# Readout gate, merge gates and both branch products with tokens on the output partitions

## The chip, the cores and the metric

The kernel runs on one core of a Trainium2 chip. The time is what one execution takes on the device in microseconds (us). TensorE (PE) multiplies: it loads a stationary operand of 128x128 (PEld) and streams a moving operand of up to 512 columns through it, into a PSUM bank. There are eight banks of 128 x 512 in fp32. DVE is VectorE, ACT is ScalarE, POOL is GpSimd and SP is the queue that issues most of the loads.

## The reference

One layer of a diffusion backbone on 256 latent tokens with 256 context tokens, width 2048, all in fp32. What matters here, with `h` the normed and modulated latent tokens and `p_g`, `p_gc`, `p_gh` columns of the one input projection `h @ w_in`:

```
o = rms_norm(o, hgrn_norm_g)                      # per head of 128
y_h = (o * silu(p_g)) @ hgrn_out_w                # 1024 -> 2048, "who"
y_c = silu(layer_norm(conv(u))) @ conv_pw_w       # 1024 -> 2048, "wpw"
z = sigmoid(p_gc) * y_c + sigmoid(p_gh) * y_h
y = z @ w_out                                     # 2048 -> 2048, "wo"
x = x + ga_m * rms_norm(y, norm_post_mix)         # then the squared-ReLU MLP, 2048 -> 8192 -> 2048
```

## The kernel before

Each fp32 operand is split into a high part (rounded to `fp32r`) and a low part, and a product takes three terms: high x high, high x low and low x high. Weights come from HBM as tiles of 128 x 1024 (512 KB). For each tile ACT writes the high part (`whi`, L84) and DVE the low part (`wlo`, L85). `Stream.next` (L87 on) prepares them four tiles ahead (`AHEAD`), with four buffers each for `whi` and `wlo` and five for the raw tile. Between the weights the stream carries tiles of the modulation weights (`add_gemv`, the side stream), each of which is consumed by one DVE instruction (L779 or L790).

There are two ways of multiplying. In `blocks`, a block of 128 output features is the stationary operand and the 256 tokens move. `mm2` multiplies the high weight with high and low tokens side by side (512 columns, L197) and then the low weight with the high tokens (256 columns, L198), so the bank holds two halves of 256 that `total` adds up: an ACT copy (L176) and a DVE add (L177). In `tokens`, 128 tokens are the stationary operand and 512 weight columns move. `mm3r` issues three matmuls of 512 columns (L203 to L205) for two halves of the tokens and two halves of the tile, in four banks. A group is one pass over all the input features for 1024 output features. Its last three tiles (`LAST`; six at the end of a chain, `END`) are run bank by bank, so that the first banks are complete while the last ones are still being filled. The second MLP product and `wo` were already done this way.

The stages around the change run in this order: the conv gate and the conv value, the readout gate `g` (8 blocks of 128 features), the merge gates for conv and hgrn (16 blocks each), `who` (16 blocks with 8 input blocks), `wpw` (the same), and `wo`. In the first three of the changed stages the moving or stationary operand is `hlat`, the latent tokens; `who` reads the readout's result `self.rp`, `wpw` the conv branch's result `self.cv`. Both lie in the first halves of the pages that hold the latent tokens.

Background work is written as generators and lets itself be advanced by `pump(us)`: a pump adds a credit, and each step that a generator yields costs some of it. At most three generators (`LIVE`) are advanced. In this stretch they are the conv branch (steps of four DVE instructions, L990, at 1.6 a step, then a layer norm with two means on TensorE, L1013), two readouts of four heads each (with transposes on TensorE, L973), and gain rows that follow a completed side product (L828). `finish` advances one to its end. A planner puts each engine's instructions in order from these priorities and its own estimate of durations. An engine runs its queue in that order. `page` gives one of 30 buffers of 128 x 1024; the loads of x for the residual (L633, on the POOL queue) wait for four of them to be free.

Of the kernel before, what the change touches and what calls it, by code (L numbers as in the profile page):

```python
# [8 lines left out]
F32 = mybir.dt.float32  # L9
# [6 lines left out]
P = 128  # L16
# [79 lines left out]
class Kernel:  # L96
# [141 lines left out]
    def tokens(self, x, evac, us, end=False):  # L238


        for g in range(2):
            n = KT - (END if end and g else LAST)
            accs = [self.bank() for _ in range(4)]

            def part(w, k, tb, j):
                xh, xl = x(k)[:2]
                t, c = slice(tb * P, (tb + 1) * P), slice(j * 512, (j + 1) * 512)
                self.mm3r(accs[2 * tb + j], (xh[:, t], xl[:, t]), (w[0][:, c], w[1][:, c]), k == 0, k == KT - 1)
            for k in range(n):
                w = self.stream.next(AHEAD)  # L250
                for tb in range(2):
                    for j in range(2):
                        part(w, k, tb, j)
                self.pump(us)
            ws = [self.stream.next(min(AHEAD, KT - k) if end and g else AHEAD) for k in range(n, KT)]
            for tb in range(2):
                for j in range(2):
                    for k, w in enumerate(ws):
                        part(w, n + k, tb, j)
            for tb in range(2):  # L260
                for j in range(2):
                    evac(tb, 2 * g + j, accs[2 * tb + j])
            self.pump(us)
# [22 lines left out]
    def run(self):  # L286
# [91 lines left out]
        for b in [*range(40, 48), *range(32, 40), *range(24, 32), *range(48, 80)]:  # L378
            w_in(b)
            if b % 7 < 3:  # L380
                gemv(1)
# [201 lines left out]
        def ev_g(b, accs):  # L583
            acc = self.totals(accs, self.small(512, "sum"))
            sg = self.small(512, "sg")
            nc.scalar.activation(out=sg, in_=acc, func=AF.Sigmoid)
            for j in range(2):
                s = slice(j * T, (j + 1) * T)
                nc.vector.scalar_tensor_tensor(self.at(self.sg, b + j), acc[:, s], v["hng"][:, b + j:b + j + 1], sg[:, s], op0=ALU.mult, op1=ALU.mult)

        self.blocks(8, hlat, KT, ev_g, 1.1)
# [4 lines left out]
        gp = [[], []]  # L596

        def ev_gate(i):
            def ev(b, accs):
                if b % PB == 0:  # L600
                    gp[i].append(self.page(F32, "gate"))
                acc = self.totals(accs, self.at(gp[i], b, 2))
                nc.scalar.activation(out=acc, in_=acc, func=AF.Sigmoid)
            return ev

        self.blocks(16, hlat, KT, ev_gate(0), 1.1)
        self.blocks(16, hlat, KT, ev_gate(1), 1.1)
# [4 lines left out]
        def ev_ho(b, accs):  # L612
            acc = self.totals(accs, self.small(512, "sum"))
            y = self.at(gp[1], b, 2)
            nc.vector.tensor_tensor(y, acc, y, op=ALU.mult)

        self.blocks(16, self.operand(self.rp), 8, ev_ho, 1.2)
# [3 lines left out]
        def ev_pw(b, accs):  # L621
            acc = self.totals(accs, self.small(512, "sum"))
            z, y = self.at(gp[0], b, 2), self.at(gp[1], b, 2)
            nc.vector.tensor_tensor(z, acc, z, op=ALU.mult)
            nc.vector.tensor_tensor(z, z, y, op=ALU.add)
            self.split(z, self.at(zh, b, 2), self.at(zl, b, 2))

        self.blocks(16, self.operand(self.cv), 8, ev_pw, 1.2)


# [38 lines left out]
        self.tokens(zx, ev_wo, 1.4, end=True)  # L669
# [287 lines left out]
    def readout(self, j):  # L957

        nc = self.nc
        while self.ended < 4 * (j + 1):  # L960
            yield None
        r = self.osq[:, 8 * j:8 * j + 8]
        self.rstd(r, r, 1.0 / P)
        for h in range(4 * j, 4 * j + 4):
            o = self.at(self.on, h)
            for tb in range(2):
                s = o[:, tb * P:(tb + 1) * P]
                nc.vector.tensor_scalar(out=s, in0=s, scalar1=self.osq[:, 2 * h + tb:2 * h + tb + 1], scalar2=None, op0=ALU.mult)
            yield 0.4
            yield None  # L970
            ps = self.bank()
            for tb in range(2):
                nc.tensor.transpose(out=ps[:, tb * P:(tb + 1) * P], in_=o[:, tb * P:(tb + 1) * P], identity=self.v["ident"])  # L973
            nc.vector.tensor_tensor(o, ps[:, :T], self.at(self.sg, h), op=ALU.mult)
            self.split_parts(o, self.rp, h, 1)
            yield 0.8

    def conv(self, uhv, uvv):
# [74 lines left out]
       ("wm0", (64, P, TW), F32), ("crow", (2, TW), F32), ("wmt", (64, P, TW), F32), ("wm1", (64, P, TW), F32), ("wi0", (16, P, TW), F32), ("wi1", (160, P, TW), F32),  # L1053
       ("wpw", (16, P, TW), F32), ("who", (16, P, TW), F32), ("wo", (32, P, TW), F32), ("w1", (128, P, TW), F32), ("w2", (128, P, TW), F32)]
# [76 lines left out]
```

## Time and profile before

| | us |
|---|---|
| median of 3 runs | 1710.58 (1710.08 to 1710.60) |
| profiled execution | 1710.51 |
| its span, first to last instruction | 1708.7 |
| PE busy | 1669.4 |
| PEld busy | 1418.5 |
| DVE busy | 1205.3 |
| ACT busy | 869.9 |
| DMA | 374.61 MB, mean 219 GB/s |

The page's share of busy time is an average over stages with different limits. A matmul's row shows its duration with what overlaps the next one, so a pace is read from the distance of two starts in the timeline. "Idle before" is the time that an engine stood still ahead of an instruction, and the name behind the arrow is what ended it.

### The profile page before, as it was taken

The page shows a single profiled execution, that of the slowest core. Times are in us where ns is not written, and L with a number is a line of the kernel's source. Part 1 is how long each engine was busy: PE and PEld are TensorE (multiplying, and loading weights), DVE is VectorE, ACT ScalarE, POOL GpSimd, SP SyncE. Part 2 cuts the span into 40 slices and gives each one's busy share as a digit, 9 for nine tenths or more (in the row PEclk, how much of TensorE's full clock was granted, in tenths as well). Part 3 has the DMA queues.
Part 4 walks back from the last instruction along what each step waited for, and adds up shares of the span by engine and source line. Part 5 has one row for each costly group of instructions (what it writes and reads, how often), then busy time and mean ns, then how long its engine had stood idle before and what let it go on. Part 6 is the DMA issues. An engine that isn't in the chain of part 4 may idle for free.

```text
span 1708.7 us, 24005 instructions
## 1 busy us (share of the span) xinstructions
PE 1669.4 (98%) x9082; PEld 1418.5 (83%) x9082; DVE 1205.3 (71%) x1688; ACT 869.9 (51%) x1260; POOL 8.1 (0%) x18
## 2 busy tenths in 40 slices
PE   4999999999999999999999999999999999999997
PEld 2777887888888888888888898888888888888886
DVE  6887767777676999997797566555665665556555
ACT  8785333344454444574455466445553455345542
POOL 0000000000000000000000000000000000000000
PEclk9999999999999999999999999999999999999999
DMA  8887985433356677668887466767666666766553
GB/s 326 309 298 283 335 270 166 148 124 111 99 166 205 208 236 237 221 215 277 294 268 260 150 209 221 213 227 229 219 216 218 233 221 211 228 219 196 193 190 120
DMA packets 103348, 374.61 MB, mean 219 GB/s; under 512 B 11584, under 2 KB 11584, under 8 KB 103232
## 3 DMA queue, kind: packets, MB, share of 16 engines
q1 hardware_dynamic: 101952, 368.86, 65.2%
q0 software_dynamic: 1280, 4.21, 0.7%
q8 instruction: 71, 1.16, 0.3%
q14 instruction: 45, 0.37, 0.1%
HBM read 370.93 MB, written 2.10 MB: 218 GB/s over the span
## 4 chain that ended last, share of the span: by engine, by line
PE 86%; DMA 5%; DVE 4%; ACT 3%; issue 2%; SPq 0%; DVEq 0%; ACTq 0%
PE bank L197 27%; PE bank L198 14%; PE bank L204 8%; PE bank L205 8%; PE bank L203 8%; PE bank L192 4%; PE bank L190 4%; PE bank L191 4%; DMA raw<-wm 4%; PE bank L905 2%; DVE wlo L85 2%; PE bank L849 1%; PE bank L848 1%; PE bank L847 1%; ACT whi L84 1%
## 5 line engine op out<-in xcount | busy, mean ns | idle before, releaser
L85 DVE TENSOR_TENSOR wlo<-raw,whi 128x1024 fp32r<-128x1024 f32 x547 | 665.3, 1222 | 315.3 <-ACT whi L84 309.2
L84 ACT ACTIVATE whi<-raw 128x1024 fp32r<-128x1024 f32 x547 | 575.6, 1059 | 599.5 <-PE bank L197 227.6
L197 PE MATMUL bank<-h,whi 128*128 128x512 f32 x2176 | 766.6, 397 | 0.0
L198 PE MATMUL bank<-h,wlo 128*128 128x256 f32 x2176 | 610.9, 281 | 3.3 <-DVE wlo L85 3.2
L197 PEld LDWEIGHTS bank<-h,whi 128*128 128x128 f32 x2176 | 408.3, 188 | 95.5
L198 PEld LDWEIGHTS bank<-h,wlo 128*128 128x128 f32 x2176 | 411.5, 189 | 4.9 <-DVE wlo L85 4.7
L204 PE MATMUL bank<-wlo,hidh 128*128 128x512 f32 x500 | 194.6, 389 | 0.0
L203 PE MATMUL bank<-whi,hidh 128*128 128x512 f32 x500 | 194.6, 389 | 0.0
L205 PE MATMUL bank<-whi,hidl 128*128 128x512 f32 x500 | 194.6, 389 | 0.0
L190 PE MATMUL bank<-h,whi 128*128 128x512 f32 (+1 forms) x384 | 140.7, 367 | 1.8 <-ACT whi L84 1.0
L191 PE MATMUL bank<-h,whi 128*128 128x512 f32 (+1 forms) x384 | 136.1, 355 | 0.0
L192 PE MATMUL bank<-h,wlo 128*128 128x512 f32 (+1 forms) x384 | 135.8, 355 | 0.0
L205 PEld LDWEIGHTS bank<-whi,hidl 128*128 128x128 f32 x500 | 93.9, 188 | 19.6
L203 PEld LDWEIGHTS bank<-whi,hidh 128*128 128x128 f32 x500 | 93.9, 188 | 19.5
L204 PEld LDWEIGHTS bank<-wlo,hidh 128*128 128x128 f32 x500 | 93.9, 188 | 19.3
L779 DVE SCALAR_TENSOR_TENSOR gacc<-raw,silu_c,gacc 128x1024 f32<-128x1024 f32 x60 | 76.9, 1282 | 46.3 <-DMA raw<-wm 46.0
L790 DVE SCALAR_TENSOR_TENSOR raw<-raw,silu_row 128x1024 f32<-128x1024 f32 x64 | 77.3, 1221 | 25.8 <-DMA raw<-wmt 25.8
L485 PE MATMUL bank<-whi,s 128*4 128x256 f32 x256 | 66.9, 294 | 16.8 <-ACT whi L84 16.8
L190 PEld LDWEIGHTS bank<-h,whi 128*128 128x128 f32 x384 | 72.8, 190 | 10.7 <-ACT whi L84 1.2
L192 PEld LDWEIGHTS bank<-h,wlo 128*128 128x128 f32 x384 | 72.3, 189 | 10.5 <-DVE wlo L85 0.2
L191 PEld LDWEIGHTS bank<-h,whi 128*128 128x128 f32 x384 | 72.8, 190 | 8.6 <-DVE h L185 0.3
L486 PE MATMUL bank<-wlo,s 128*4 128x256 f32 x256 | 66.0, 291 | 6.9 <-DVE wlo L85 6.3
(203 smaller groups left out, 1538.5 us busy)
## 6 DMA issues: line engine op xcount, KB each, us to landing
raw<-w SPq DMA_DIRECT2D x256, 512.0 KB, 4.2
raw<-wi SPq DMA_DIRECT2D x176, 512.0 KB, 4.3
raw<-wm SPq DMA_DIRECT2D x128, 512.0 KB, 4.6
raw<-wmt SPq DMA_DIRECT2D x64, 512.0 KB, 4.4
raw<-wo SPq DMA_DIRECT2D x32, 512.0 KB, 4.5
raw<-who SPq DMA_DIRECT2D x16, 512.0 KB, 4.7
raw<-wpw SPq DMA_DIRECT2D x16, 512.0 KB, 4.5
x<-x SPq DMA_DIRECT2D x4, 512.0 KB, 7.3
```

The lines of the kernel that those rows point to most:

```text
L84: nc.scalar.activation(out=hi, in_=raw, func=AF.Copy)
L85: kn.los.append(nc.vector.tensor_tensor(lo, raw, hi.bitcast(F32), op=ALU.subtract))
L190: nc.tensor.matmul(out, w[0], x[0], start=first, stop=False)
L191: nc.tensor.matmul(out, w[0], x[1], start=False, stop=False)
L192: nc.tensor.matmul(out, w[1], x[0], start=False, stop=last)
L197: nc.tensor.matmul(bank, w[0], x[2], start=first, stop=False)
L198: nc.tensor.matmul(bank[:, T:], w[1], x[0], start=False, stop=last)
L203: nc.tensor.matmul(out, x[0], w[0], start=first, stop=False)
L204: nc.tensor.matmul(out, x[0], w[1], start=False, stop=False)
L205: nc.tensor.matmul(out, x[1], w[0], start=False, stop=last)
L779: nc.vector.scalar_tensor_tensor(acc, raw, s, acc, op0=ALU.mult, op1=ALU.add)
L790: nc.vector.scalar_tensor_tensor(raw, raw, 1.0, self.srow, op0=ALU.mult, op1=ALU.mult, accum_out=self.dot[:, 32 * j + b:32 * j + b + 1])
```

## The change

The readout gate, the merge gates and the products `who` and `wpw` go from `blocks` to `tokens`. Their weights are laid out in rows (new input `wi2`, and `who` and `wpw` by `rows`). `tokens` gets the number of input blocks (`nk`), the number of groups, another order of the four banks (`pairs`) and a hook before a tile (`pre`). The gates are now evacuated from the bank by one sigmoid. The norm gain moves from the gate's evacuation to the readout, and the gate is multiplied before the readout's transpose instead of after it. The merged result z has tokens on partitions, so `turn_z` transposes it in eight steps of four 128x128 transposes, four steps during the second group of `wpw` and four during the first group of `wo`, and splits each step's bank into high and low part. The pumps of these stages have 1.3 in place of 1.1 and 1.2, one per tile outside the last three, and one per group. The order of `w_in` columns in the stream and the places of the side stream's tiles are rewritten to fit. The cut hunk declares the shapes of the inputs.

```diff
--- before.py
+++ after.py
@@ -235,31 +235,33 @@
             evac(2 * j, accs[j])
         self.pump(us)
-    def tokens(self, x, evac, us, end=False):
-        for g in range(2):
-            n = KT - (END if end and g else LAST)
+    def tokens(self, x, evac, us, end=False, nk=KT, groups=2, pairs=False, pre=None):
+        order = [(tb, j) for j in range(2) for tb in range(2)] if pairs else [(tb, j) for tb in range(2) for j in range(2)]
+        for g in range(groups):
+            last = end and g == groups - 1
+            n = nk - (END if last else LAST)
             accs = [self.bank() for _ in range(4)]
             def part(w, k, tb, j):
                 xh, xl = x(k)[:2]
                 t, c = slice(tb * P, (tb + 1) * P), slice(j * 512, (j + 1) * 512)
-                self.mm3r(accs[2 * tb + j], (xh[:, t], xl[:, t]), (w[0][:, c], w[1][:, c]), k == 0, k == KT - 1)
+                self.mm3r(accs[2 * tb + j], (xh[:, t], xl[:, t]), (w[0][:, c], w[1][:, c]), k == 0, k == nk - 1)
             for k in range(n):
+                if pre is not None:
+                    pre(g, k)
                 w = self.stream.next(AHEAD)
-                for tb in range(2):
-                    for j in range(2):
-                        part(w, k, tb, j)
+                for tb, j in order:
+                    part(w, k, tb, j)
                 self.pump(us)
-            ws = [self.stream.next(min(AHEAD, KT - k) if end and g else AHEAD) for k in range(n, KT)]
-            for tb in range(2):
-                for j in range(2):
-                    for k, w in enumerate(ws):
-                        part(w, n + k, tb, j)
-            for tb in range(2):
-                for j in range(2):
-                    evac(tb, 2 * g + j, accs[2 * tb + j])
+            ws = [self.stream.next(min(AHEAD, nk - k) if last else AHEAD) for k in range(n, nk)]
+            for tb, j in order:
+                for k, w in enumerate(ws):
+                    part(w, n + k, tb, j)
+            for tb, j in order:
+                evac(tb, 2 * g + j, accs[2 * tb + j])
             self.pump(us)
     def cut(self, pages, tb, c):
@@ -375,9 +377,13 @@
             gemv(1 + (h + 1) % 2)
             w_in(8 + h)
             gemv(1 + (h + 1) % 2)
-        for b in [*range(40, 48), *range(32, 40), *range(24, 32), *range(48, 80)]:
+        for b in [*range(32, 40), *range(24, 32)]:
             w_in(b)
             if b % 7 < 3:
+                gemv(1)
+        for b in range(80):
+            st.add(a["wi2"][b])
+            if b % 14 < 6 and b % 2 == 0:
                 gemv(1)
         for nm in ("who", "wpw"):
             for b in range(16):
@@ -580,52 +586,65 @@
         self.sg = self.pages(2, F32, "silu_g")
-        def ev_g(b, accs):
-            acc = self.totals(accs, self.small(512, "sum"))
-            sg = self.small(512, "sg")
-            nc.scalar.activation(out=sg, in_=acc, func=AF.Sigmoid)
-            for j in range(2):
-                s = slice(j * T, (j + 1) * T)
-                nc.vector.scalar_tensor_tensor(self.at(self.sg, b + j), acc[:, s], v["hng"][:, b + j:b + j + 1], sg[:, s], op0=ALU.mult, op1=ALU.mult)
-        self.blocks(8, hlat, KT, ev_g, 1.1)
+        def ev_g(tb, c, acc):
+            s = self.sg[tb][:, c * 512:(c + 1) * 512]
+            nc.scalar.activation(out=s, in_=acc, func=AF.Sigmoid)
+            nc.vector.tensor_tensor(s, acc, s, op=ALU.mult)
+        self.tokens(hlat, ev_g, 1.3, groups=1)
         for j in range(2):
             heads.append(self.push(self.readout(j)))
-        gp = [[], []]
+        gp = [[None] * 4, [None] * 4]
         def ev_gate(i):
-            def ev(b, accs):
-                if b % PB == 0:
-                    gp[i].append(self.page(F32, "gate"))
-                acc = self.totals(accs, self.at(gp[i], b, 2))
-                nc.scalar.activation(out=acc, in_=acc, func=AF.Sigmoid)
+            def ev(tb, c, acc):
+                if c % 2 == 0:
+                    gp[i][2 * tb + c // 2] = self.page(F32, "gate")
+                nc.scalar.activation(out=self.cut(gp[i], tb, c), in_=acc, func=AF.Sigmoid)
             return ev
-        self.blocks(16, hlat, KT, ev_gate(0), 1.1)
-        self.blocks(16, hlat, KT, ev_gate(1), 1.1)
+        self.tokens(hlat, ev_gate(0), 1.3)
+        self.tokens(hlat, ev_gate(1), 1.3)
         for g in heads:
             self.finish(g)
-        def ev_ho(b, accs):
-            acc = self.totals(accs, self.small(512, "sum"))
-            y = self.at(gp[1], b, 2)
+        def ev_ho(tb, c, acc):
+            y = self.cut(gp[1], tb, c)
             nc.vector.tensor_tensor(y, acc, y, op=ALU.mult)
-        self.blocks(16, self.operand(self.rp), 8, ev_ho, 1.2)
+        self.tokens(self.operand(self.rp), ev_ho, 1.3, nk=8)
         self.finish(conv)
         zh, zl = self.pages(4, F32R, "zh"), self.pages(4, F32R, "zl")
-        def ev_pw(b, accs):
-            acc = self.totals(accs, self.small(512, "sum"))
-            z, y = self.at(gp[0], b, 2), self.at(gp[1], b, 2)
+        def ev_pw(tb, c, acc):
+            z, y = self.cut(gp[0], tb, c), self.cut(gp[1], tb, c)
             nc.vector.tensor_tensor(z, acc, z, op=ALU.mult)
             nc.vector.tensor_tensor(z, z, y, op=ALU.add)
-            self.split(z, self.at(zh, b, 2), self.at(zl, b, 2))
-        self.blocks(16, self.operand(self.cv), 8, ev_pw, 1.2)
+        def turn_z():
+            for k in range(0, KT, 2):
+                ps = self.bank()
+                for j in range(2):
+                    o = (k + j) % 8 * P
+                    for tb in range(2):
+                        nc.tensor.transpose(out=ps[:, j * T + tb * P:j * T + (tb + 1) * P], in_=gp[0][2 * tb + k // 8][:, o:o + P], identity=v["ident"])
+                self.split(ps, self.at(zh, k, 2), self.at(zl, k, 2))
+                yield
+        zturn = turn_z()
+        def pre_pw(g, k):
+            for _ in range(2 * (g == 1 and k > 2)):
+                next(zturn)
+        def pre_wo(g, k):
+            if g == 0 and 2 < k < 7:
+                next(zturn)
+        self.tokens(self.operand(self.cv), ev_pw, 1.3, nk=8, pairs=True, pre=pre_pw)
         xr = self.pages(4, F32, "xr")
@@ -666,7 +685,7 @@
             st.behind = [[sqrt, scaled[0]]]
         zx = lambda k: (self.at(zh, k), self.at(zl, k))
-        self.tokens(zx, ev_wo, 1.4, end=True)
+        self.tokens(zx, ev_wo, 1.4, end=True, pre=pre_wo)
         h2 = self.parts(KT, "h2")
         turn = self.turn([yp], True, [A2], [mv[:, 0]], [h2])
         next(turn)
@@ -965,15 +984,17 @@
             o = self.at(self.on, h)
             for tb in range(2):
                 s = o[:, tb * P:(tb + 1) * P]
-                nc.vector.tensor_scalar(out=s, in0=s, scalar1=self.osq[:, 2 * h + tb:2 * h + tb + 1], scalar2=None, op0=ALU.mult)
-            yield 0.4
+                nc.vector.scalar_tensor_tensor(s, s, self.osq[:, 2 * h + tb:2 * h + tb + 1], self.sg[tb][:, h * P:(h + 1) * P], op0=ALU.mult, op1=ALU.mult)
+            yield 0.5
             yield None
             ps = self.bank()
             for tb in range(2):
                 nc.tensor.transpose(out=ps[:, tb * P:(tb + 1) * P], in_=o[:, tb * P:(tb + 1) * P], identity=self.v["ident"])
-            nc.vector.tensor_tensor(o, ps[:, :T], self.at(self.sg, h), op=ALU.mult)
-            self.split_parts(o, self.rp, h, 1)
-            yield 0.8
+            g = self.v["hng"][:, h:h + 1]
+            hi, lo = self.rp[h][:, :T], self.rp[h][:, T:]
+            nc.scalar.activation(out=hi, in_=ps[:, :T], func=AF.Copy, scale=g)
+            nc.vector.scalar_tensor_tensor(lo, ps[:, :T], g, hi.bitcast(F32), op0=ALU.mult, op1=ALU.subtract)
+            yield 0.5
     def conv(self, uhv, uvv):
         nc, v = self.nc, self.v
...
@@ -1112,9 +1133,10 @@
         "wmt": wm[:, 3 * D:5 * D].T.reshape(32, P, 2, TW).transpose(2, 0, 1, 3).reshape(-1, P, TW),
         "wm1": np.stack([wm[:, 2 * D:3 * D], wm[:, 5 * D:]]).reshape(2, KT, P, 2, TW).transpose(0, 1, 3, 2, 4).reshape(-1, P, TW),
         "wi0": row(wi[:, :DH]),
-        "wi1": cb(wi[:, DH:]),
-        "wpw": cb(f(conv_pw_w)[0]),
-        "who": cb(f(hgrn_out_w)[0]),
+        "wi1": cb(np.concatenate([wi[:, DH:4 * DH], wi[:, 5 * DH:7 * DH]], axis=1)),
+        "wi2": np.concatenate([wi[:, 4 * DH:5 * DH].reshape(KT, P, TW), rows(wi[:, 7 * DH:9 * DH]), rows(wi[:, 9 * DH:])], axis=0),
+        "wpw": rows(f(conv_pw_w)[0]),
+        "who": rows(f(hgrn_out_w)[0]),
         "wo": rows(f(w_out)[0]),
         "w1": np.concatenate([both(w1[:, :D]), cb(w1[:, D:])], axis=0),
         "w2": np.concatenate([rows(w2[i * D:(i + 1) * D]) for i in range(4)], axis=0),
```

## Rows read from the trace of the kernel before

**Rows 1.** Page, busy time and instructions of the engines, and the clock in 40 slices.

```profile
PE 1669.4 (98%) x9082; PEld 1418.5 (83%) x9082; DVE 1205.3 (71%) x1688; ACT 869.9 (51%) x1260; POOL 8.1 (0%) x18
...
PEclk9999999999999999999999999999999999999999
```

**Rows 2.** One tile, `zh`: count, shortest/median/longest ns, first and last start.

```profile
L203 PE MATMUL bank<-whi,zh x116: 388/389/398, 887.6 to 975.3; 128*128 128x512 f32 x116
```

**Rows 3.** Table by stretch: busy us (count) of each engine, clock, DMA share, GB/s.

```profile
565.70:698.90 133.20, 133.20 (x771) 117.48 (x770) 132.70 (x244) 64.84 (x84) 0.00 (x0) 1.00 0.71 233
...
698.90:838.20 139.30, 139.30 (x798) 121.41 (x798) 122.72 (x171) 80.67 (x125) 1.75 (x4) 1.00 0.75 242
...
838.20:887.60 49.40, 46.15 (x259) 39.21 (x258) 42.56 (x57) 22.85 (x37) 2.55 (x5) 1.00 0.85 288
...
1257.00:1301.70 44.70, 44.70 (x199) 36.99 (x198) 27.00 (x28) 19.22 (x22) 0.00 (x0) 1.00 0.66 212
...
850.00:855.00 5.00, 2.53 (x16) 1.97 (x14) 2.55 (x3) 1.32 (x2) 0.00 (x0) 1.00 0.66 244
```

**Rows 4.** Groups of instructions, 565.7 to 887.6: busy us, mean ns | idle before, releaser.

```profile
L198 PE MATMUL bank<-h,wlo 128*128 128x256 f32 x897 | 252.1, 281 | 3.3 <-DVE wlo L85 3.2
...
L85 DVE TENSOR_TENSOR wlo<-raw,whi 128x1024 fp32r<-128x1024 f32 x110 | 133.6, 1218 | 4.4 <-ACT whi L84 4.3
...
L990 DVE SCALAR_TENSOR_TENSOR conv<-uh,pack,conv 128x256 f32<-128x256 f32 x120 | 50.7, 476 | 0.0
...
L177 DVE TENSOR_TENSOR sum<-bank,terms 128x256 f32<-128x256 f32 x37 | 15.1, 416 | 0.0
...
L973 PE MATMUL bank<-pack,o 128*128 128x128 f32 x16 | 2.9, 272 | 0.0
...
L1013 PE MATMUL bank<-lnred,mean 128*128 128x256 f32 x8 | 2.0, 378 | 0.0
...
L828 PE MATMUL bank<-gpart,ones_r 128*128 128x512 f32 x4 | 1.1, 398 | 0.0
```

**Rows 5.** Chain that ended last, 560 to 900, longest pieces: start, us, what.

```profile
837.35 5.96 DMA raw<-wm
...
844.64 7.78 DMA raw<-wm
```

**Rows 6.** Timeline of POOL, 800 to 880: start, us, engine, line, instruction.

```profile
837.62 2.08 POOL L633 DMA_DIRECT2D xr<-x  x4 [67.48 <-PE bank L198]
```

**Rows 7.** Timeline of PE in the first merge gate: two starts, 28 pairs apart.

```profile
659.68 0.39 PE L197 MATMUL bank<-h,whi 128*128 128x512 f32 x1
...
669.39 0.39 PE L197 MATMUL bank<-h,whi 128*128 128x512 f32 x1
```

**Rows 8.** Timeline of PE in `wo`: two starts, 34 matmuls apart.

```profile
924.96 0.39 PE L203 MATMUL bank<-whi,zh 128*128 128x512 f32 x1
...
932.66 0.39 PE L204 MATMUL bank<-wlo,zh 128*128 128x512 f32 x1
```

**Rows 9.** Timeline of PE around one readout.

```profile
766.08 0.28 PE L198 MATMUL bank<-h,wlo 128*128 128x256 f32 x1
...
766.20 0.38 PE L973 MATMUL bank<-pack,o 128*128 128x128 f32 x2
...
766.65 0.28 PE L198 MATMUL bank<-h,wlo 128*128 128x256 f32 x1
```

**Rows 10.** Timeline of DVE around a group end of the MLP product.

```profile
1291.19 1.28 DVE L779 SCALAR_TENSOR_TENSOR gacc<-raw,silu_c,gacc 128x1024 f32<-128x1024 f32 x1 [0.80 <-DMA raw<-wm]
...
1292.40 1.22 DVE L85 TENSOR_TENSOR wlo<-raw,whi 128x1024 fp32r<-128x1024 f32 x1
...
1301.41 2.36 DVE L85 TENSOR_TENSOR wlo<-raw,whi 128x1024 fp32r<-128x1024 f32 x2 [1.08 <-ACT whi L84]
```

**Rows 11.** Timeline of PE there: first uses of those two low halves.

```profile
1294.90 0.39 PE L204 MATMUL bank<-wlo,hidh 128*128 128x512 f32 x1
...
1304.42 0.39 PE L204 MATMUL bank<-wlo,hidh 128*128 128x512 f32 x1
```

More of the change, by code (lines that the diff above doesn't have):

```diff
@@ L1052 @@
 _IN = [("pack", (P, NPACK), F32), ("x", (T, D), F32), ("ctx", (T, D), F32), ("bgain", (4, TW), F32), ("gain", (4, TW), F32), ("masks", (P, 7 * P), I32),
-       ("wm0", (64, P, TW), F32), ("crow", (2, TW), F32), ("wmt", (64, P, TW), F32), ("wm1", (64, P, TW), F32), ("wi0", (16, P, TW), F32), ("wi1", (160, P, TW), F32),
-       ("wpw", (16, P, TW), F32), ("who", (16, P, TW), F32), ("wo", (32, P, TW), F32), ("w1", (128, P, TW), F32), ("w2", (128, P, TW), F32)]
+       ("wm0", (64, P, TW), F32), ("crow", (2, TW), F32), ("wmt", (64, P, TW), F32), ("wm1", (64, P, TW), F32), ("wi0", (16, P, TW), F32), ("wi1", (80, P, TW), F32),
+       ("wi2", (80, P, TW), F32),        ("wpw", (16, P, TW), F32), ("who", (16, P, TW), F32), ("wo", (32, P, TW), F32), ("w1", (128, P, TW), F32), ("w2", (128, P, TW), F32)]
 def _masks():
```

## The prediction

> **What bounds the kernel now.** I read the page's busy times first, then the table by stretch for the part that the change touches, then the timelines of single engines inside it. TensorE is busy 98% of the span and its granted clock is full in every slice [rows 1], so a stage is worth what its matmuls are paced at, plus whatever TensorE waits for. The touched work is five stages in a row: the readout gate, the two merge gates, the hgrn product (`who`) and the conv product (`wpw`). They end where `wo` begins, with the first matmul that reads `zh`, at 887.6 us [rows 2]. Counting their 896 block steps (8, 32, 16 and 16 blocks, of 16, 16, 8 and 8 steps) backwards from there gives a start of 565.7, and the list of groups has 897 `L198` matmuls in that stretch, one of them of the stage before [rows 4]. So the change acts on 321.9 us of 1708.7.
>
> In this stretch the reader is to see two different limits. Until 838.2 TensorE is busy without a break, although DVE is at 132.70 of 133.20 us in the first 133 us [rows 3]: DVE is full there, but weights are prepared four tiles ahead and TensorE never runs out. In the `wpw` stage TensorE is busy 46.15 of 49.40 us [rows 3] and its idle time ends with DVE's low half of a weight [rows 4]. The chain that ended last goes through DMAs of the side stream there, 5.96 and 7.78 us long [rows 5]; just before them four 512 KB loads of x were issued on the POOL queue, all at 837.62 [rows 6]. In 850 to 855 TensorE has only 2.53 us of work; the clock stays at 1.00 [rows 3], so a wait of this length costs itself and nothing more.
>
> **The change part by part.**
>
> *Matmuls.* Before, one step is a 512-column matmul (high half of the weight against both halves of the tokens) and a 256-column one. Twenty-eight such pairs lie between 659.68 and 669.39 [rows 7]: 9.71/28 = 0.347 us a pair. After, the same arithmetic for two steps is a triple of 512 columns, as `wo` has it: 34 matmuls from 924.96 to 932.66 [rows 8], 0.2265 us each, 0.679 a triple. Two pairs are 0.694, so the pace alone gives 0.014 us a triple at the fastest pair pace. For all 896 pairs the total is better than a pace: 321.9 us less the foreign TensorE work in the stretch, 2.0 us of means (`L1013`), 1.1 of the gain row (`L828`) [rows 4] and 16 readout transposes at 0.11 (below), 1.8. That leaves 317.0 us, 354 ns a pair, and 3.25 of it is the idle time of `wpw`. After: 448 triples x 0.679 = 304.4 us. Difference -12.6: 3.25 is stall, 9.4 pace. Bounds: with the pace of [rows 7] alone it would be 448 x 0.014 = -6.4; with the stretch's own pace and the stall -12.6. I take the second, since it is the stretch itself.
>
> *Transposes of z.* New are 32 of 128x128 (8 steps of four). The nearest row is the readout's: from the `L198` at 766.08 to the next one at 766.65 is 0.57 us with two transposes and one 512-column matmul between, against 0.347 for the normal pair [rows 9]: 0.11 a transpose. 32 x 0.11 = +3.5 us, all on TensorE and so on the path; upper bound by the mean duration of `L973`, 272 ns [rows 4], 8.7. The lower one is 32 x 0.11, since nothing on TensorE can hide them. [...]
>
> *Evacuations.* Before, each of the 72 blocks had its two bank halves added up: an ACT copy and a DVE add of 0.416 us (the "sum" group of `L177` [rows 4], the gates' being the same shape). These go. The gates need one sigmoid from the bank; the products keep their multiplies; the readout loses one DVE operation and one ACT pass a head. Cost on the path: nothing before 838, as TensorE never waited for DVE there. It is DVE's slack that changes. Background work is metered by credits: g and gates had 80 pumps of 1.1 (88), now 14 a group in five groups at 1.3 (91). A 16-tile group of gates costs DVE 44.2 us now (132.70/3); less 8 adds (some 0.34 each where the next instruction starts before the end), 2.7, plus 3% more of the conv's 18 us, 0.6, is 42 against 43.5 of TensorE: 97%. In `wpw` DVE has 42.56 us, less 16 adds (5.4) and half the splits, against 43.5: 80 to 85%. So the DVE queue that made TensorE wait in `wpw` is gone, if the loads come in time.
>
> *Order of the stream.* The same 512 KB tiles and the same count of side-stream tiles between them; SP's queue gets no more issues. The x loads on POOL still wait for pages that the hgrn product's operand leaves, so they still land on the border of `who` and `wpw`. I count their crowd as part of the next term.
>
> *Group ends, a new wait.* `tokens` runs the last three tiles bank by bank, so three of four weight buffers are held until the end of a group. What the lead shrinks to is seen in the second product of the MLP: the last tile's low half ends at 1293.62 and its first use is at 1294.90; the low half of the next group's second tile ends at 1302.63 (1301.41 + 1.22, the first of the two in its row) and is used at 1304.42 [rows 10, 11]. That is 1.3 and 1.8 us of lead, with DVE at 27.00 of 44.70 us [rows 3], and TensorE did not wait. In the changed stages DVE has 80 to 97%, and there are nine such ends. Queued behind one another on DVE can be a conv step (4 x 50.7/120 = 1.7 us [rows 4]), a side-stream product (1.28 [rows 10]) and another low half (1.22 [rows 4]): 4.2 us against 1.8 of lead, so at most 2.4 us an end, 21.6 in all; at least nothing. I take 0.6 at the five ends of g and gates and 0.25 at the four others: +4.0 us, nearer to zero, because background work isn't issued during those three tiles.
>
> *The transposes' own waits.* TensorE runs in order, so a transpose whose z isn't ready holds all matmuls behind it. The first needs two evacuations that can start about 6 us before the group ends and is issued three tiles (8.2 us) after it. I count it at nothing; without that cover it would be 1 to 1.5 us at each of the six places.
>
> **Sum:** -12.6 + 3.5 + 4.0 = -5.1 us. The profiled execution took 1710.51 us, 1.81 more than its span, and lies 0.07 under the median of 1710.58, so the two are the same here: 1710.5 - 5.1 = 1705.4 us.
>
> **The rivals.**
>
> *A. The lead at group ends decides (slower).* DVE late at every end. Break-even is (12.6 - 3.5)/9 = 1.0 us an end; over 1.4 us an end it is slower by more than 0.2%. At 2.4 us: 1710.5 - 9.1 + 21.6 = 1723. For it: DVE without idle time in the first 133 us [rows 3]. Against it: the adds go, and nothing is pumped in the last three tiles. Chance 0.12.
>
> *B. The loads of x keep their stall.* The 3.25 us stay as a wait for late weights. 1705.4 + 3.3 = 1708.7. For it: same four loads, same place [rows 6]. Against it: five raw tiles are loaded by the time a group ends, and the DVE queue is shorter. Chance 0.15.
>
> *C. Columns alone count.* Two pairs and one triple have the same 1536 columns, so the 9.4 us of pace would not come: 1705.4 + 9.4 = 1714.8. For it: only that tokens-as-stationary with these operands isn't in the trace at full length. Against it: the two paces, 0.694 and 0.679 [rows 7, 8]. Chance 0.05. [...]
>
> *D. TensorE held by the transposes.* Six places at 1 us: 1711. Chance 0.08.
>
> **How the numbers follow.** Forecast 0.60, A 0.12, B 0.15, C 0.05, D 0.08. About 0.2% (3.4 us) is what a measurement of this kernel can tell from no change, so faster means under 1707.2. Forecast gives faster 0.60; B, D and the lower half of C and A's mild end give the same, 0.25; the rest of A and C slower, 0.15. The forecast's own range is 1701 (no waits at the ends, -9.1) to 1707.2. The whole range goes to 1716, into A at 1.6 us an end: 1700.5 to 1716.
>
> **What would show it.** In the profile after, the stretch from the gate to `wo` should be 313 to 317 us. The triple reading `h` should keep 0.2265 us a matmul, and a group of four transposes cost 0.44. TensorE's idle time with DVE's low half as releaser should stand at group ends, below 6 us in all; above 9 us A is right. If the matmuls of the conv product still wait some 3 us about 10 us after the four x loads, B is. If the pace is 0.23 and more a matmul, C. A wait of a transpose for DVE's z or for a bank would be D.

## The result, and the profile after

The changed kernel takes 1713.79 us (median of 12 runs, 1710.64 to 1715.37) against 1710.35 for the kernel before in the same runs: a ratio of 1.002, 95% interval 1.0012 to 1.0027. It is slower by 3.4 us, where 5 us faster was forecast. The profiled execution has a span of 1712.2 us against 1708.7.

The columns of the first view are as in [rows 3]. It shows the changed kernel's five stages: gate and merge gates, then `who`, then `wpw`, and last the 4.8 us after the longest wait in `wpw`.

```profile
566.00:788.10 222.10, 221.89 (x987) 182.97 (x986) 196.82 (x309) 112.03 (x135) 1.17 (x2) 1.00 0.73 233
788.10:839.70 51.60, 46.38 (x198) 36.31 (x196) 34.94 (x35) 17.92 (x20) 2.12 (x4) 1.00 0.81 283
839.70:889.40 49.70, 47.22 (x210) 38.77 (x209) 41.62 (x46) 18.51 (x21) 1.05 (x2) 0.97 0.79 275
...
881.20:886.00 4.80, 4.80 (x15) 3.77 (x16) 3.87 (x5) 0.00 (x0) 0.00 (x0) 0.64 0.79 246
```

The gates gained what their pace promised: 222.1 us, where the kernel before took 226.5 from 565.7. `who` lost it again. TensorE is idle 5.2 of 51.60 us there and DVE is busy for only 34.94. In `wpw` TensorE is idle 2.5 us and then runs at a granted clock of 0.64 on average. The next stage, `wo`, has 1.5 us more, about what 16 of the new transposes cost.

The groups of instructions from 788.1 to 889.4 have the answer to `L198` and `L85` of [rows 4]. `L798` is the side product (`L779` before), `L634` the transpose of z.

```profile
L204 PE MATMUL bank<-wlo,h 128*128 128x512 f32 x128 | 51.1, 399 | 7.1 <-DVE wlo L85 7.1
L85 DVE TENSOR_TENSOR wlo<-raw,whi 128x1024 fp32r<-128x1024 f32 x32 | 38.1, 1218 | 0.7 <-ACT whi L84 0.6
...
L798 DVE SCALAR_TENSOR_TENSOR gacc<-raw,silu_c,gacc 128x1024 f32<-128x1024 f32 x16 | 20.5, 1283 | 22.1 <-DMA raw<-wm 21.9
L634 PE MATMUL bank<-pack,gate 128*128 128x128 f32 x16 | 2.1, 272 | 0.0
```

The reader is to see two idle times together: TensorE waits 7.1 us for low halves, and DVE, which makes them, stands still for 22.1 us ahead of side products whose tile hasn't landed. DVE isn't full. It is blocked. It was so before, but less: the same group of side products over all five stages, first in the kernel before (565.7 to 887.6), then in the changed one (566 to 889.4).

```profile
L779 DVE SCALAR_TENSOR_TENSOR gacc<-raw,silu_c,gacc 128x1024 f32<-128x1024 f32 x25 | 32.0, 1280 | 17.2 <-DMA raw<-wm 17.0
```

```profile
L798 DVE SCALAR_TENSOR_TENSOR gacc<-raw,silu_c,gacc 128x1024 f32<-128x1024 f32 x27 | 34.6, 1283 | 28.9 <-DMA raw<-wm 28.7
```

The matmuls, counted from the start of each stage, tell where TensorE's four waits for a low half stand. Call the last three tiles of a group, which are run bank by bank, its tail. At 792.88 and 816.30 (1.69 and 1.05 us) TensorE waits for the second tile of the group behind a tail, at 832.99 and 881.07 (1.86 and 2.48 us) for the last tile of a tail, in its first bank. The next four views show the first of these waits: the timelines of DVE, ACT, SP and PE.

```profile
783.31 1.28 DVE L798 SCALAR_TENSOR_TENSOR gacc<-raw,silu_c,gacc 128x1024 f32<-128x1024 f32 x1 [3.58 <-DMA raw<-wm]
784.51 1.22 DVE L85 TENSOR_TENSOR wlo<-raw,whi 128x1024 fp32r<-128x1024 f32 x1
790.41 1.29 DVE L798 SCALAR_TENSOR_TENSOR gacc<-raw,silu_c,gacc 128x1024 f32<-128x1024 f32 x1 [4.68 <-DMA raw<-wm]
791.61 4.63 DVE L85 TENSOR_TENSOR wlo<-raw,whi 128x1024 fp32r<-128x1024 f32 x4
```

```profile
786.93 2.01 ACT L84 ACTIVATE whi<-raw 128x1024 fp32r<-128x1024 f32 x2
```

```profile
785.76 0.33 SPq L71 DMA_DIRECT2D raw<-wm  x1
```

```profile
790.81 0.39 PE L203 MATMUL bank<-whi,h 128*128 128x512 f32 x1
792.88 0.50 PE L204 MATMUL bank<-wlo,h 128*128 128x512 f32 x1 [1.69 <-DVE wlo L85]
```

The first low half could have been made once its high half was there, at 788.0 at the latest (786.93 and half of 2.01). It stands behind the side product of 790.41 in DVE's queue, which waits for a load that was issued at 785.76, just when the low half of 784.51 gave a raw buffer back (784.51 + 1.22 = 785.73). That low half had itself waited behind the side product of 783.31. So here a late side product delays the low half behind it, that half frees its raw buffer late, and the next side load starts late.

### The profile page after: what moved, and what is told of

It reads as the page before. It is cut to its first block, busy times and chain, and to the rows that moved or that the text cites. A ratio compares the mean times of both kernels' runs of the same rounds, so it can differ in the third digit from the quotient of the medians.

```text
span 1712.2 us, 23007 instructions
## 1 busy us (share of the span) xinstructions
PE 1670.5 (98%) x8666; PEld 1400.7 (82%) x8666; DVE 1179.7 (69%) x1604; ACT 851.2 (50%) x1188; POOL 8.1 (0%) x18
## 4 chain that ended last, share of the span: by engine, by line
PE 81%; DVE 7%; DMA 6%; ACT 3%; issue 3%; SPq 0%; DVEq 0%; ACTq 0%
PE bank L197 17%; PE bank L204 12%; PE bank L205 11%; PE bank L203 11%; PE bank L198 9%; DMA raw<-wm 5%; PE bank L192 4%; PE bank L190 4%; PE bank L191 4%; DVE wlo L85 4%; PE bank L924 2%; ACT whi L84 1%; PE bank L866 1%; PE bank L867 1%; PE bank L868 1%
## 5 line engine op out<-in xcount | busy, mean ns | idle before, releaser
L85 DVE TENSOR_TENSOR wlo<-raw,whi 128x1024 fp32r<-128x1024 f32 x547 | 664.3, 1223 | 327.9 <-ACT whi L84 321.9
L197 PE MATMUL bank<-h,whi 128*128 128x512 f32 x1280 | 452.5, 398 | 0.0
L198 PE MATMUL bank<-h,wlo 128*128 128x256 f32 x1280 | 359.0, 280 | 0.0
L197 PEld LDWEIGHTS bank<-h,whi 128*128 128x128 f32 x1280 | 240.3, 188 | 57.3
L198 PEld LDWEIGHTS bank<-h,wlo 128*128 128x128 f32 x1280 | 241.8, 189 | 0.2
L203 PE MATMUL bank<-whi,hidh 128*128 128x512 f32 x500 | 194.5, 389 | 0.0
L205 PE MATMUL bank<-whi,hidl 128*128 128x512 f32 x500 | 194.5, 389 | 0.0
L204 PE MATMUL bank<-wlo,h 128*128 128x512 f32 x448 | 175.9, 393 | 7.3 <-DVE wlo L85 7.2
L203 PE MATMUL bank<-whi,h 128*128 128x512 f32 x448 | 175.3, 392 | 0.0
L205 PE MATMUL bank<-whi,h 128*128 128x512 f32 x448 | 175.0, 391 | 0.0
L798 DVE SCALAR_TENSOR_TENSOR gacc<-raw,silu_c,gacc 128x1024 f32<-128x1024 f32 x60 | 77.0, 1284 | 59.9 <-DMA raw<-wm 59.7
L203 PEld LDWEIGHTS bank<-whi,hidh 128*128 128x128 f32 x500 | 93.8, 188 | 19.7
L205 PEld LDWEIGHTS bank<-whi,hidl 128*128 128x128 f32 x500 | 93.8, 188 | 19.5
L204 PEld LDWEIGHTS bank<-wlo,h 128*128 128x128 f32 x448 | 84.4, 188 | 27.3 <-DVE wlo L85 10.2
L203 PEld LDWEIGHTS bank<-whi,h 128*128 128x128 f32 x448 | 84.5, 189 | 17.5
L205 PEld LDWEIGHTS bank<-whi,h 128*128 128x128 f32 x448 | 84.5, 189 | 17.4
```

The source lines that it names most:

```text
L85: kn.los.append(nc.vector.tensor_tensor(lo, raw, hi.bitcast(F32), op=ALU.subtract))
L197: nc.tensor.matmul(bank, w[0], x[2], start=first, stop=False)
L198: nc.tensor.matmul(bank[:, T:], w[1], x[0], start=False, stop=last)
L203: nc.tensor.matmul(out, x[0], w[0], start=first, stop=False)
L204: nc.tensor.matmul(out, x[0], w[1], start=False, stop=False)
L205: nc.tensor.matmul(out, x[1], w[0], start=False, stop=last)
```

## The experiments

Each is timed against the kernel before on the same chip. The kernel before took 1709.49 us beside the first four of the runs under the changed kernel, 1710.49 beside the next four and 1709.68 beside the last three, so rows of different rounds are best compared by their ratios. The stage lengths are worked out from the starts of the first matmuls of the stages in each run's trace. "Gates" is the readout gate and both merge gates. "Lost" below is what `who` and `wpw` take beyond 44.5 and 45.3 us, their lengths in the runs where TensorE doesn't wait in them: 11.5 us in the changed kernel, 7.7 of it idle time.

| run | median, us | ratio (95%) | gates | `who` | `wpw` | `wo` |
|---|---|---|---|---|---|---|
| before | 1710.35 | 1 | 226.5 | 45.9 | 49.4 | 88.4 |
| changed | 1713.79 | 1.002 (1.0012 to 1.0027) | 222.1 | 51.6 | 49.7 | 89.9 |
| side tiles out | 1712.29 | 1.0013 (1.0004 to 1.0023) | 229.1 | 43.5 | 45.9 | 94.1 |
| side products without loads | 1704.33 | 0.9966 (0.9954 to 0.9978) | 222.2 | 44.5 | 45.3 | 92.2 |
| short tail | 1707.39 | 0.9984 (0.9975 to 0.9993) | 222.2 | 46.2 | 47.0 | 90.6 |
| before, side tiles out | 1710.94 | 1.0009 (1.0 to 1.0017) | 235.2 | 44.4 | 44.4 | 89.2 |
| other order on DVE | 1707.18 | 0.9978 (0.9969 to 0.9986) | 222.2 | 46.6 | 47.0 | 89.9 |
| before, other order | 1710.74 | 1.0002 (0.9993 to 1.0011) | 226.5 | 46.1 | 48.4 | 90.6 |
| short tail in all stages | 1707.39 | 0.9983 (0.9973 to 0.9992) | 225.3 | 44.5 | 46.2 | 90.2 |
| other order and short tail | 1703.28 | 0.9958 (0.9945 to 0.997) | 221.8 | 44.5 | 45.3 | 89.9 |
| smaller pools (control) | 1713.76 | 1.0022 (1.0013 to 1.0032) | 222.1 | 51.3 | 47.5 | 90.0 |
| the same, six raw buffers | 1713.86 | 1.0021 (1.0011 to 1.003) | 226.8 | 45.0 | 51.4 | 91.1 |
| other order in the gates too | 1701.81 | 0.9953 (0.9939 to 0.9968) | 221.9 | 44.5 | 45.3 | 89.9 |

**Side tiles out of `who` and `wpw`.**

```diff
         for nm in ("who", "wpw"):
             for b in range(16):
                 st.add(a[nm][b])
-                if b % 2 == 0:
-                    gemv(1)
# and in the gates: if b >= 48 and b % 16 in (3, 5, 7, 9, 11): gemv(1)
```

> The changed kernel with the 16 side-stream tiles taken out of who and wpw: ten go into the second merge gate, six into wo. Theory 1 (a side product that waits for its own late load stands on DVE ahead of a weight's low half): the waits of TensorE for low halves in who and wpw, 11.5 us, fall under 2 us, and the slow clock behind the last of them goes too: 1702 to 1706 us. Theory 2 (the weight buffers held to the end of a group leave too little lead, whatever is queued): the waits at the group ends stay at 6 us or more, 1708 to 1713. Theory 3 (the four loads of x crowd the DMA): some 3 us stay in wpw, 1706 to 1708.

In `who` and `wpw` the waits went as theory 1 had it (43.5 and 45.9 us, with `who`'s gain row of 0.9 us moved to the gates as well), but the time didn't. 1712.29 lies in the range of theory 2, whose waits at the group ends did not stay: the waits moved with the tiles. The gates lost 7 us and `wo` 4. In the second merge gate DVE came late with the readouts and with a gain row, and TensorE stood in its queue at the readouts' transposes (`L992`, idle for 1.94 us; the seven matmuls from 734.87 follow at 0.426 us in place of 0.227, the pace of the lower clock in the changed kernel's `wpw`) and, for 1.29 us, at the gain row. The timeline of PE in that run:

```profile
731.65 0.39 PE L203 MATMUL bank<-whi,h 128*128 128x512 f32 x1
733.98 0.50 PE L992 MATMUL bank<-pack,o 128*128 128x128 f32 x2 [1.94 <-DVE o L987]
...
736.15 0.63 PE L203 MATMUL bank<-whi,h 128*128 128x512 f32 x1
```

**Side products without loads.**

```diff
+        if ap is None:
+            fn(kn.accv[:, :TW])
+            return
         raw = kn.wp.tile([P, TW], F32, name="raw", tag="raw", bufs=5)
# who, wpw:  st.add_gemv(None, gq.popleft()[1])
```

> The changed kernel with the 16 side products of who and wpw kept on DVE at their places, at the same size, but without their loads: each reads its own accumulator, so the gains of the first residual are not the reference's. Theory 1: the waits go as in the run without side tiles, 1702 to 1705 us. If the work on DVE itself is what is too much (16 x 1.28 us), the waits stay, 1711 to 1714. If it is the hold of the weight buffers (theory 2), 1708 to 1713.

1704.33, in the range of theory 1. It is 9.5 us under the changed kernel: 11.5 won in `who` and `wpw`, 2.3 lost in `wo`, which begins with a wait at its own first side tiles, as these still have loads. The groups of that run in the two stages, with no wait of TensorE:

```profile
L207 PE MATMUL bank<-wlo,h 128*128 128x512 f32 x128 | 49.8, 389 | 0.0
...
L801 DVE SCALAR_TENSOR_TENSOR gacc<-gacc,silu_c 128x1024 f32<-128x1024 f32 x9 | 11.5, 1278 | 0.1
```

The tail is as in the changed kernel, so the hold of the weight buffers isn't a cause by itself. About DVE's work the run says less: without loads to wait for, six of the sixteen products ran ahead, between 764 and 776 in the second merge gate, and DVE was busy for 70.0 us in the two stages against 76.6 in the changed kernel. Nor does it tell the load's wait on DVE from what these 8 MB do to the other loads.

**Short tail.** One tile bank by bank instead of three, in `who` and `wpw` (and `pre_pw` limited to the same four steps).

```diff
-            n = nk - (END if last else LAST)
+            n = nk - (END if last else LAST if nk == KT else 1)
```

> The changed kernel with only the last tile of a group run bank by bank in who and wpw (three before), side tiles where they were. Theory 1 in its full form (held weight buffers hold the raw buffers, so the side tile's load is issued late) : waits fall from 11.5 to some 3 us, 1704 to 1708. If the side tile's load is late for another reason, they stay, 1712 to 1715. If the short tail makes TensorE wait for banks instead, waits for a bank appear at the group ends, 1 us each.

In time as theory 1 in its full form: 6.4 us less than the changed kernel, 3.4 lost where it was 11.5. The tail is thus part of the cause, though not alone. But the way that this theory gave for it isn't what the trace shows. The side loads don't start earlier (the one of 785.76 in the changed kernel is issued at 785.72 here), and DVE waits for them at least as long (25.7 us against 22.1). The groups of that run, 785 to 884:

```profile
L204 PE MATMUL bank<-wlo,h 128*128 128x512 f32 x134 | 52.9, 394 | 1.8 <-DVE wlo L85 1.8
...
L798 DVE SCALAR_TENSOR_TENSOR gacc<-raw,silu_c,gacc 128x1024 f32<-128x1024 f32 x15 | 19.2, 1282 | 25.7 <-DMA raw<-wm 25.7
```

What the short tail gives back is lead. Tile by tile in the traces, DVE begins a low half 2.0 us after its high half is done on average in the changed kernel, and 2.9 us after it here, so the block is no smaller. But from the end of the high half to the tile's first use the second tile of the second group of `who` has 4.3 us in the changed kernel and 7.1 here, and the last tile of that stage's first group 3.2 and 7.1. A tail of three begins its three tiles within about 2 us (three triples) and gives their buffers back within 1.4 us of its end, so less lead is left to hide the block.

**The kernel before, side tiles out.**

```diff
         for nm in ("who", "wpw"): ...
-                if b % 2 == 0:
-                    gemv(1)
# and in the gates: if b >= 64 and b % 8 in (1, 2, 3, 4, 5): gemv(1)
```

> The kernel before with the same 16 side tiles taken out of who and wpw. Theory 1: its own 3.3 us of idle TensorE in wpw go as well, 1706 to 1707.5 us, so the change beats it by less than it beats the kernel as it was. Theory 3 (loads of x): they stay, 1710.

A miss in the sum. `wpw` lost its stall (44.4 for 49.4), but the gates grew by 8.6 us, 5.9 of it idle time where TensorE again stood at the readout's transposes. In both kernels moving the side tiles only moved the wait.

**Other order on DVE.** In `who`, `wpw` and `wo` the side product is issued behind the low half of the next weight tile, with the same loads.

```diff
         if fn is not None:
-            fn(raw)
+            if paged:
+                self.held.append((raw, fn))
+            else:
+                fn(raw)
             return
...
             kn.los.append(nc.vector.tensor_tensor(lo, raw, hi.bitcast(F32), op=ALU.subtract))
+            for raw, fn in self.held:
+                with kn.tc.issue_after(kn.los[-1].ins):
+                    fn(raw)
+            self.held = []
```

> The changed kernel; in who, wpw and wo the side product's DVE instruction is issued behind the low half of the weight tile that follows it in the stream. Same loads, same work, same three tiles bank by bank; only the order on DVE differs. Theory 1 (a side product waiting for its load blocks the low half behind it): the waits of 11.5 us in who and wpw fall under 3 us, 1703 to 1706 us. If late loads of the weights themselves are the cause, or the hold of the buffers alone, the waits stay: 1711 to 1714.

The two stages lose 3.8 us (2.1 in `who`, 1.7 in `wpw`), a little over the 3 that were expected, and the time fell to 1707.18, over the 1703 to 1706 of theory 1. Its profiled execution is at 1705.4. Loads, bytes and DVE work are the same, so the order alone carries two thirds of the loss. DVE now begins a low half 0.6 us after its high half on average, against 2.0. The groups of the two stages:

```profile
L212 PE MATMUL bank<-wlo,h 128*128 128x512 f32 x128 | 50.3, 393 | 0.9 <-DVE wlo L89 0.9
...
L806 DVE SCALAR_TENSOR_TENSOR gacc<-raw,silu_c,gacc 128x1024 f32<-128x1024 f32 x15 | 19.2, 1278 | 0.0
L855 PE MATMUL bank<-gpart,ones_r 128*128 128x512 f32 x4 | 1.6, 450 | 1.1 <-DVE gpart L193 1.1
```

No side product waits for its load any more. What is left is TensorE's wait for the parts of a gain row (`L855`), and a few late low halves.

**The kernel before, other order** (the same edit there).

> The kernel before with the same other order on DVE. Theory 1 for its own 3.3 us of idle time in wpw: they go, 1706 to 1708 us. If that idle time comes from DVE having too much work there (the halves' adds), it stays, 1709 to 1711. It also says what the change is worth when neither kernel has the block: by the stage table of the changed kernel, some 3 to 5 us.

The stall in `wpw` stays in the main (48.4), `wo` is 2.2 us longer, and the time is the same. So the kernel before loses at most 1 us of its stall to this block: its side products there no longer wait, and TensorE still waits 2.3 us for low halves. As the stall went with the side tiles, and the high halves wait 14.9 us for late `wpw` tiles in that run's profile, the side tiles' loads are the likeliest cause, but that wasn't tested by itself.

**Short tail in all stages** (gate, merge gates, `who`, `wpw` and the first group of `wo`).

> The changed kernel with one tile bank by bank instead of three in all five changed stages and in the first group of wo; side tiles and order as they were. Against the run with one in who and wpw alone (1707.4): the wait of 1.1 us at the first tiles of who goes, since the gates' last group holds no buffers either: 1705 to 1708. If the short tail delays the evacuations so much that banks are missing at the group ends of the gates, 1709 or more.

The wait at the first tiles of `who` went (44.5), as expected. The gates lost 3.2 us: the planner put a readout's transposes earlier, and TensorE was idle 1.7 us at one, waiting for DVE. The other 1.5 are close to the 1.6 us that the lower clock cost in the changed kernel's `wpw`, but no view of that run shows the clock. In sum no change against the short tail in two stages.

**Other order and short tail.**

> Both remedies: the side product behind the next low half in who, wpw and wo, and one tile bank by bank in these stages. Theory 1: the block is gone with the order alone, so the shorter tail adds under 1.5 us to it: 1702 to 1705. If the hold has a cost of its own, this run is 2 us or more under the order alone.

The short tail here covers the second merge gate, `who`, `wpw` and the first group of `wo`. Both remedies together leave no wait of TensorE for a low half in `who` and `wpw`. The groups, and the table of the two stages:

```profile
L212 PE MATMUL bank<-wlo,h 128*128 128x512 f32 x128 | 49.8, 389 | 0.0
...
L806 DVE SCALAR_TENSOR_TENSOR gacc<-raw,silu_c,gacc 128x1024 f32<-128x1024 f32 x15 | 19.2, 1278 | 0.0
```

```profile
788.60:833.10 44.50, 44.50 (x198) 36.82 (x197) 32.28 (x32) 17.93 (x20) 2.31 (x4) 1.00 0.89 306
833.10:878.40 45.30, 45.30 (x210) 37.69 (x209) 38.42 (x42) 19.52 (x21) 1.05 (x2) 1.00 0.85 295
```

It is 3.9 us under the order alone, more than the 1.5 expected, so the hold has a cost of its own. DVE begins a low half 0.4 us after its high half, and the second tiles of both groups of `who` have 7.1 us from the high half to the first use, against 3.05 in the run with the order alone. The version beats both kernels.

**Six raw buffers, and its control.** Room for the sixth came from one buffer less in each of two pools of small tiles; the control has these with five raw buffers.

> Control for the next run: the changed kernel with one buffer less in each of the two pools of small tiles (four of 512, five of 256 columns), five raw buffers. Nothing of the theory changes: waits of 9 to 13 us in who and wpw, 1711 to 1715.

> The same with six raw buffers. If the side tile's load is late because a raw buffer comes free late, a sixth lets it be issued one tile earlier (some 2.7 us): waits in who and wpw fall from 11.5 to under 6 us, 1706 to 1710. If the load is late because the DMA is full, or only the order on DVE matters, they stay, 1711 to 1715.

In time the control is as the changed kernel; its `wpw` is 2.1 us shorter, its longest wait there being 1.90 us. The stage is 2.2 us over the 45.3 without waits, which leaves no room for another 1.6 of a lower clock behind that wait. The sixth buffer emptied `who` of waits (45.0) and moved them: the end of the second merge gate has a wait of 2.76 us, and the matmuls from 783.90 behind it follow at 0.427 us (the gates are 4.7 us longer), and `wpw` is 3.9 us longer than in the control. The time is unchanged, so the number of raw buffers isn't the remedy. The same block stands in the DVE timeline of that run, and PE's wait behind it:

```profile
834.54 1.28 DVE L798 SCALAR_TENSOR_TENSOR gacc<-raw,silu_c,gacc 128x1024 f32<-128x1024 f32 x1 [5.98 <-DMA raw<-wm]
...
840.22 1.28 DVE L798 SCALAR_TENSOR_TENSOR gacc<-raw,silu_c,gacc 128x1024 f32<-128x1024 f32 x1 [2.06 <-DMA raw<-wm]
841.42 0.68 DVE L616 TENSOR_TENSOR gate<-bank,gate 128x512 f32<-128x512 f32 x1
842.02 2.35 DVE L85 TENSOR_TENSOR wlo<-raw,whi 128x1024 fp32r<-128x1024 f32 x2
```

```profile
843.29 0.50 PE L204 MATMUL bank<-wlo,h 128*128 128x512 f32 x1 [3.27 <-DVE wlo L85]
```

**Other order in the gates too.**

> The run with both remedies (1703.3), and the side products of the gate stages behind the next low half as well. There is only 0.4 us of waiting for low halves left in the gates, so 1702.5 to 1704 if the theory holds; if the order costs something of its own, 1705 or more.

1701.81, with stage lengths like those of the run with other order and short tail, which this one builds on. The two medians differ by less than their intervals, so this run says only that the order costs nothing there.

## Why the prediction was wrong

*Matmuls: right in mechanism and size.* 304.4 us of triples, 4.9 of foreign work and 1.8 of transposes in `wpw` were 311.1 us from the gate to `wo`. With the waits taken away this stretch lasts 311.6 (other order and short tail). The split of the 12.6 us is off, though: the gates gained 4.4 us for 640 of the 896 pairs, near the pace of [rows 7] that was set aside, and the stall in `wpw` was worth 5.0 us (49.4 against 44.4 without side tiles), not 3.25. The pace of a triple was 0.6806 us in the readout gate. Rival C is out.

*Transposes of z: right.* In the run without waits `wpw` takes 45.3 us for 64 triples of 0.680 us (the pace in `wpw` of the changed kernel, 841 to 865), 43.5, so 16 transposes cost 1.8, 0.11 each. The row of `L634` shows 272 ns as the duration of one, but eight that start at 873.24 stand between the matmul at 873.00 and the second one behind them at 874.34: 1.34 us less two matmuls of 0.227 is again 0.11 each, and that decides on the path.

*Evacuations: right.* In the gates TensorE is idle 0.2 us of 222.1. DVE's share there is 89%, and up to 96% in a single group (41.84 of 43.5 us), where 97% was expected.

*Order of the stream: wrong.* "The same 512 KB tiles and the same count of side-stream tiles between them" was taken as no cost. The count is the same, what the tiles cost on DVE isn't: its idle time ahead of side products grew from 17.2 to 28.9 us over the five stages. Why it grew isn't shown; the short tail left it as it was.

*Group ends: the term that failed.* It was set at 0.25 us for each of the four ends in `who` and `wpw`, 1.0 in all, and at most 2.4 each. The bound counted what DVE has to do (conv step, side product, low half) and not what it waits for. The places were right: the two leads of [rows 10, 11], 1.3 us for a tail's last tile and 1.8 for the next group's second, are those at which TensorE waited. The side product at the head of the queue waited 1 to 5 us for its load, and TensorE lost 11.5 us in these two stages, 1.6 of it by the clock below, where the term has 1.0, or 4.0 with the gates' ends (the wait at 792.88 is behind the last of these). Inside the gates, where DVE's busy share was expected to be dangerous (97%), TensorE is idle for 0.2 us. The busy share was the wrong measure. With the order on DVE turned and the tail shortened, the term is 0.2 us and the gain of the forecast's other terms comes out: 7.2 us under the kernel before (8.7 by the four stages of the table), where they alone had given 9.1. The low half of 791.61, whose high half was done by 788.0, came only behind the side product of 790.41, which had waited 4.68 us for its load: DVE took the two in the order of its queue.

*The clock: wrong in one place.* "A wait of this length costs itself and nothing more" held for the kernel before [rows 3] and for the waits in `who`, where the granted clock is 1.00. After the longest wait in `wpw` it didn't. The timeline of PE there:

```profile
878.20 0.39 PE L203 MATMUL bank<-whi,h 128*128 128x512 f32 x1
881.07 0.50 PE L204 MATMUL bank<-wlo,h 128*128 128x512 f32 x1 [2.48 <-DVE wlo L85]
...
882.58 0.63 PE L204 MATMUL bank<-wlo,h 128*128 128x512 f32 x1
883.01 0.63 PE L205 MATMUL bank<-whi,h 128*128 128x512 f32 x1
```

Eight matmuls from 882.58 follow at 0.427 us instead of 0.227: the granted clock is 0.50 from 883.00 to 885.50, and they take 1.6 us more.

*The rivals.* A had the sign and about the amount (11.5 us are 1.3 an end over nine ends), but not the reason: it saw DVE as full and late at every end, and DVE was idle 17 of 51.6 us in `who`, while the first four of the gates' five ends cost next to nothing. 1713.79 lies in the whole range of 1700.5 to 1716 only through A, so that is luck. The sign that was to tell them apart, TensorE's idle time behind DVE's low halves, came to 7.2 us, between the 6 of the forecast and the 9 of A. B's loads of x were issued between 822 and 827 and are beside one of the waits (the 1.86 us that end at 832.99), but with both remedies the same loads cost nothing. D, a wait at the transposes of z, showed in no stage of the changed kernel; what TensorE waited for in three other runs were the readouts' transposes, with the matmuls behind them (with the side tiles out 1.94 us up to 733.98, and the next matmul at 734.23). In sum the other terms were close, and the one that was bounded from too few causes carried the sign.

What stays open: why DVE waits longer for side loads than in the kernel before; how much of the hold's own 3.9 us (order alone against both) is the lead itself, and how much is the gain row's parts coming late. And that the planner expects side loads sooner than they land, which would explain why it puts the product ahead of the low half, was not measured.

## What to carry to other kernels

Here DVE starved TensorE while it stood idle itself: in `who` and `wpw` it was idle for 22.1 us ahead of side products, and TensorE waited 7.1 us for its low halves. So look at what ended an engine's idle time, and price a queue by the waits of the instructions in it, not only by their work. An instruction that needs a load of its own belongs behind the work that others wait for: with that order alone these two stages lost 3.8 us in place of 11.5. When a loop is changed so that it holds buffers to the end, look at the lead of the work that is prepared ahead: two tiles of `who` had 4.3 and 3.2 us with a tail of three and 7.1 with a tail of one, and the two stages lost 11.5 and 3.4 us. Moving the loads behind such waits to another stage moved the waits with them here: the gates took 7.0 us more and `wo` 4.2.

## What the runs showed of the hardware

In `wpw` of the changed kernel the granted clock fell to 0.50, and matmuls came at 0.427 us in place of 0.227, after TensorE had been idle for 2.48 us. That pace followed as well after 1.94 us (0.426; side tiles out, at a readout) and 2.76 us (0.427; six raw buffers, second merge gate). It didn't after 2.47 us (kernel before, `wpw`: the clock is 1.00 from 850 to 860) and 3.27 us (six raw buffers, `wpw`: `L203` and `L205` have means of 391 and 390 ns in `who` and `wpw`, against 390 and 389 with both remedies). After 1.94 us at the start of `wo` (side tiles out) the matmuls from 890.02 to 890.72 come at 0.23 to 0.24 us, and after 1.90 us in `wpw` of the control the stage's length leaves no room for it. So in these runs the length of the idle time didn't decide by itself.

The pair of a 512- and a 256-column matmul had two paces in the kernel before: 0.347 us in the readout gate and the first merge gate (567 to 698), 0.353 from 720 us on in the second merge gate and in the second quarter of the MLP (1168 to 1256). In `wpw` it had 0.347 once its side tiles were gone (44.37 us for 128 pairs). What sets it wasn't tested. The triple of 512 had 0.680 us in the first merge gate, `wpw` and `wo` of the changed kernel and in `wo` and the second MLP product of the kernel before, 0.681 in the readout gate.
